# The same start address, 448 modulo 1024 bytes, for every activation operand that streams against the weights of a two-layer decoder trunk

## The chip, the cores and the metric

The kernel runs on one core of one Trainium2 chip. Its time is the device time of one execution in microseconds (us). A core has a matrix engine (TensorE, PE in the rows; PEld is its weight load), two elementwise engines (VectorE, DVE; ScalarE, ACT), GpSimd (POOL) and SyncE (SP), which issues the transfers. They work in parallel and wait for each other through semaphores. On-chip memory (SBUF) has 128 partitions; an address here is the byte offset within a partition. TensorE accumulates into PSUM.

## The reference

Two decoder layers over 256 tokens and 1024 channels, all in float32. Layer 0 mixes with block attention and a state-space scan side by side, layer 1 with a gated delta rule; after each mixer comes a gated feed-forward part and a gated embedding:

```python
for i in range(DEPTH):                      # DEPTH = 2
    h = rmsnorm(x, norm_mix[i])
    x = x + (even_mixer(h, ...) if i % 2 == 0 else gdn_mixer(h, ...))
    h = rmsnorm(x, norm_ffn[i])
    x = x + conv_ffn(h, ...)                # (silu(conv(h @ w_gate)) * (h @ w_up)) @ w_down, width 2816
    x = x + per_layer_embedding(x, p[i], ...)   # sigmoid(rmsnorm(x) @ w_gate) * (p[i] @ w_proj)
```

Every projection is a product of a (channels x tokens) activation with a weight matrix; there are about 34 million weights.

## The kernel before

**Tiling.** Activations lie with channels on the partitions: a 1024-channel activation is 8 tiles of 128 x 256 (channels x tokens), each 1024 bytes per partition. The weights lie in one stream in the order of their use. `piece` loads up to 1024 columns of it (512 KB) into a `raw` buffer and splits it: `whi` is the value rounded to the matmul's fp32r type by ScalarE (line 155), `wlo` the rest by VectorE (line 156). Four buffers each of `raw`, `whi` and `wlo` go round.

**The product.** Activations are split in the same way by `split` (lines 207 to 212) into a high and a low tile. `mm3` (lines 181 to 183) then does three matmuls for each 128 x 128 weight block: high weights with the high tile, high weights with the low tile, low weights with the high tile. The weight block is the stationary operand; the activation tile, 256 columns, is the moving one. Each of the three loads its own weights.

**The moving tiles and their names.** `xh`, `xl`: the normalized residual, 8 pairs (lines 224, 225); they lie in the pool that lives through the whole program, except for the ones that feed the embedding gate (`pgt`), which lie in the feed-forward part's own pool. `yh`, `yl`: the 22 pairs in the middle of the feed-forward part (lines 294, 295). `ah`, `al`: attention's output, 4 pairs (lines 640, 641). `qT`, `kT`, `sl`: the state-space output, 8 pairs, in buffers that held queries and keys before (lines 676, 677). `gh`, `gl`: the delta rule's output, 16 pairs (lines 988, 989). `ph`, `pl`: the embedding's 2 pairs, which take a buffer each of the `whi` and `wlo` rings (lines 318 to 321).

**The outputs.** In PSUM: `pg`, `pu` (gate, up), `pd` (down: 8 tiles of 22 blocks each), `pp` (embedding projection), `pgt` (embedding gate), `pxbc`, `pz`, `pqk` (layer 0's mixer inputs), `pgd`, `pz` (layer 1's), `pwa`, `pws` (layer 0's mixer output from attention and state space), `pwo` (layer 1's mixer output).

**Counts.** 6192 matmuls come from `mm3`. `pg` and `pu`: 2112 in both layers. `pd`: 1056. `pgt`: 384. `pp`: 96. `pwo`: 384, half of them in the middle of the mixer. `pws`: 192. `pwa`: 96. The inputs of the two mixers: 1872.

**Order.** A scheduler puts the instructions in order for each engine; splits of weights are moved ahead of other work (lines 153 to 156).

Of the kernel before, what the change touches and what calls it, by code (L numbers as in the profile page):

```python
# [8 lines left out]
F32R = mybir.dt.float32r  # L9
# [7 lines left out]
P = 128  # L17
BLK = 1024
# [3 lines left out]
T = 256  # L22
D = 1024
KD = D // P
DFF = 2816
NF = DFF // P
# [24 lines left out]
class Trunk:  # L51
    def __init__(self, ctx, tc, stream, xT, pT, pv, tok, cst, out):
# [12 lines left out]
        self.chain = ""  # L65
        self.nrm = ep(tc.tile_pool(name="nrm", bufs=1, space=PSUM))

        warm = self.cpool.tile([P, 1], F32, tag="warm", name="warm")
        nc.vector.memset(warm, 0.0)
        nc.scalar.activation(warm, warm, AF.Exp)  # L70
# [28 lines left out]
    def v(self, name, i=0):  # L99
        o, _ = PV[name]  # L100
        return self.pv[:, o + i:o + i + 1]

    def uid(self, s):
        self.n += 1
        return f"{s}_{self.n}"
# [107 lines left out]


    def norm_begin(self, gain, pool=None):
        self.ngain, self.npool = gain, pool or self.cpool
        self.nss = None
        self.a = [None] * KD

    def norm_tile(self, m, late=False):  # L220
        nc = self.nc
        if m == KD - 1 and not late:
            self.norm_square(m)
        xh = self.npool.tile([P, T], F32R, tag=f"xh{m}", name=self.uid("xh"), bufs=1)
        xl = self.npool.tile([P, T], F32R, tag=f"xl{m}", name=self.uid("xl"), bufs=1)
        self.split(self.x[m], xh, xl, self.v(self.ngain, m))
        self.a[m] = (xh, xl)
        if m < KD - 1 and not late:
            self.norm_square(m)
# [40 lines left out]
    def ffn(self, i, nxt):  # L270
        nc, tc = self.nc, self.tc
        with self.psum(acc=7), tc.tile_pool(name=f"ffn{i}", bufs=3) as fp:
            ys = []
            for f in range(NF):
                wg, wu = self.piece([("ffn_w_gate", i, 0, KD, f * P, P), ("ffn_w_up", i, 0, KD, f * P, P)])
                pg, pu = self.acc("pg"), self.acc("pu")
# [10 lines left out]
                sl = fp.tile([P, T], F32, tag="sl", name=self.uid("sl"))  # L287
# [3 lines left out]
                        nc.scalar.activation(self.zb[0][f], self.ident.unsqueeze(1).to_broadcast([P, 4, P]), AF.Copy)  # L291
                y = fp.tile([P, T], F32, tag="y", name=self.uid("y"))
                nc.vector.tensor_tensor(y, sl, pu[:, :T], op=ALU.mult)
                yh = fp.tile([P, T], F32R, tag=f"yh{f}", name=self.uid("yh"), bufs=1)
                yl = fp.tile([P, T], F32R, tag=f"yl{f}", name=self.uid("yl"), bufs=1)
                self.split(y, yh, yl)
                ys.append((yh, yl))
            self.norm_begin(f"ple{i}", fp)
# [15 lines left out]
    def ple_proj(self, i, pool):  # L314
        nc = self.nc
        raw = self.rawp.tile([P, BLK], F32, tag="raw", name=self.uid("raw"))
        nc.sync.dma_start(raw[:, :2 * T], self.pT[:, i].rearrange("p k t -> p (k t)"))
        ph = self.splp.tile([P, BLK], F32R, tag="whi", name=self.uid("ph"))
        pl = self.splp.tile([P, BLK], F32R, tag="wlo", name=self.uid("pl"))
        self.split(raw[:, :2 * T], ph[:, :2 * T], pl[:, :2 * T])  # L320
        pa = [(ph[:, k * T:(k + 1) * T], pl[:, k * T:(k + 1) * T]) for k in range(2)]
        self.pp = []
        ws = self.piece([("ple_w_proj", i, 0, 2, m * P, P) for m in range(KD)])
        for m in range(KD):
            ps = self.acc("pp")
            self.mm3(ps[:, :T], ws[m], pa)
            t = pool.tile([P, T], F32, tag=f"pp{m}", name=self.uid("pp"), bufs=1)
            nc.scalar.activation(t, ps[:, :T], AF.Copy, scale=0.5)
            self.pp.append(t)
# [84 lines left out]
    def _even(self, mp):  # L414
# [3 lines left out]
        KEEP = lambda shape, tag, dt=F32: mp.tile(shape, dt, tag=tag, name=self.uid(tag), bufs=1)  # L418
# [70 lines left out]
        gm = []  # L489
        for g in range(2):  # L490
# [4 lines left out]
            t = KEEP([P, 3, P], f"gm{g}")  # L495
# [42 lines left out]
        qT, kT = [], []  # L538
# [52 lines left out]
        for k0 in range(0, 8, 2):  # L591
            (wh, wl), = self.piece([(W, 0, k0, 2, 1024, 512)])
            for c in range(2):
                for k in range(2):
                    ah, al = self.a[k0 + k]
# [7 lines left out]


        aA = []
        def attend(hp):
            po = self.nrm.tile([P, 512], F32, tag="nrm", name=self.uid("po"))
            for e in range(2):
# [28 lines left out]
                PE.matmul(po[rows, 0:P], vh(0), pT[:, 0:P], start=True, stop=True)  # L637
                PE.matmul(po[rows, P:T], vh(0), pT[:, P:2 * P], start=True, stop=False)
                PE.matmul(po[rows, P:T], vh(1), pT[:, 2 * P:], start=False, stop=True)
            ah = KEEP([P, T], f"ah{hp}", F32R)  # L640
            al = KEEP([P, T], f"al{hp}", F32R)
            self.split(po[:, :T], ah, al)
            aA.append((ah, al))

# [6 lines left out]
        for g in range(2):  # L651
# [18 lines left out]
            t = self.small(2)  # L670
# [2 lines left out]
            Rg = self.replicate(rg, 2)  # L673
            for m in range(4 * g, 4 * g + 4):
                V.tensor_tensor(ytiles[m], ytiles[m], Rg[:, :T], op=ALU.mult)
                ah = KEEP([P, T], f"qT{m}" if m < 4 else f"kT{m - 4}", F32R)
                al = KEEP([P, T], f"sl{m}", F32R)
                self.split(ytiles[m], ah, al, self.v("snorm", m))
                aS.append((ah, al))

# [22 lines left out]
    def _odd(self, mp):  # L703
# [62 lines left out]

        cw = lambda t: (lambda j: self.v("gcw", t * 4 + j))
        ao = []

        def conv_tile(w, t, dst):  # L770
            ps = self.acc("pgd")
# [212 lines left out]
        def gate(kh, oT, zs):  # L984
            for e in range(2):
                z = zs[e]
                V.tensor_tensor(z, z, oT[:, e * T:(e + 1) * T], op=ALU.mult)
                ah = KEEP([P, T], f"gh{(2 * kh + e) % 16}", F32R)
                al = KEEP([P, T], f"gl{(2 * kh + e) % 16}", F32R)
                self.split(z, ah, al, nh)  # L990
                ao.append((ah, al))

# [151 lines left out]
```

## Time and profile before

| | us |
|---|---|
| median of 3 runs | 938.79 |
| lowest, highest | 937.0, 942.94 |
| the profiled execution's own time | 941.01 |
| its span, first to last instruction | 939.2 |

How to read the rows: a row of the timeline gives the start of an instruction in us from the start of the span, its recorded duration, engine, line, operation, and output tile <- input tiles. Matmuls overlap in the pipeline, so the recorded duration of one (0.28 us) is longer than the distance from its start to the start of the next. That distance is called the pitch here. It is found from two starts that lie far apart and the number of matmuls between them, which the loops give.

### The profile page before, as it was taken

The numbers are of one execution on the slowest core, as the hardware profiler recorded it, in microseconds if no ns is written. First come the engines' busy times: TensorE is split into PE (matmuls) and PEld (weight loads), VectorE is DVE, ScalarE is ACT, GpSimd is POOL, SyncE is SP. The second block draws the span as 40 slices with busy tenths as digits, with TensorE's granted clock in tenths as the row PEclk, the third lists the DMA queues.
The fourth block names the chain that finished last, engine by engine and source line by source line (L and its number), as shares of the span: only waits on it lengthen the run. The fifth ranks groups of instructions, "written<-read, shape, count | busy, mean of one in ns | idle before, by whom it ended". The sixth has DMA issues, their size and how long they took to land.

```text
span 939.2 us, 19988 instructions
## 1 busy us (share of the span) xinstructions
PE 910.0 (97%) x7834; PEld 870.1 (93%) x7834; DVE 750.1 (80%) x1636; ACT 583.7 (62%) x1235; POOL 74.3 (8%) x77
## 2 busy tenths in 40 slices
PE   8999999999999999999899999999999999999997
PEld 6988778999999999988899888988999999999997
DVE  6976778988888666889989999989678777776665
ACT  6576565666655544667688767876656555554452
POOL 0000112100000011012101111011001000000100
PEclk9999999999999999999999999999999999999999
DMA  7543323556656555554422332334445565655561
GB/s 274 183 128 113 113 91 115 158 178 202 195 189 195 180 182 174 184 154 128 146 69 79 103 114 69 111 93 113 136 138 178 180 193 189 183 181 177 172 198 68
DMA packets 40990, 141.40 MB, mean 151 GB/s; under 512 B 4672, under 2 KB 6208, under 8 KB 40896
## 3 DMA queue, kind: packets, MB, share of 16 engines
q1 hardware_dynamic: 40608, 139.84, 48.1%
q8 instruction: 61, 1.00, 0.4%
q10 hardware_dynamic: 288, 0.29, 0.1%
q14 instruction: 33, 0.27, 0.1%
HBM read 139.06 MB, written 1.05 MB: 149 GB/s over the span
## 4 chain that ended last, share of the span: by engine, by line
PE 78%; DVE 15%; ACT 4%; issue 2%; POOL 1%; DMA 0%; POOLq 0%; DVEq 0%
PE pd L183 4%; PE pd L181 4%; PE pd L182 4%; PE pg L181 4%; PE pg L182 4%; DVE wlo L156 4%; PE pu L183 4%; PE pu L182 4%; PE pg L183 4%; PE pu L181 4%; DVE chh L366 2%; PE pgd L181 2%; PE pgd L182 2%; PE pgd L183 2%; PE pwo L182 1%
## 5 line engine op out<-in xcount | busy, mean ns | idle before, releaser
L156 DVE TENSOR_TENSOR wlo<-raw,whi 128x1024 fp32r<-128x1024 f32 (+2 forms) x266 | 322.2, 1212 | 90.5 <-ACT whi L155 88.1
L155 ACT ACTIVATE whi<-raw 128x1024 fp32r<-128x1024 f32 (+2 forms) x266 | 276.5, 1040 | 179.1 <-PE pd L182 44.8
L183 PE MATMUL pd<-yh,wlo 128*128 128x256 f32 x352 | 99.6, 283 | 0.0
L181 PE MATMUL pd<-yh,whi 128*128 128x256 f32 x352 | 99.6, 283 | 0.0
L182 PE MATMUL pd<-yl,whi 128*128 128x256 f32 x352 | 99.6, 283 | 0.0
L181 PE MATMUL pg<-xh,whi 128*128 128x256 f32 x352 | 98.2, 279 | 0.6 <-DVE x L694 0.3
L181 PE MATMUL pu<-xh,whi 128*128 128x256 f32 x352 | 98.2, 279 | 0.0
L182 PE MATMUL pg<-xl,whi 128*128 128x256 f32 x352 | 98.2, 279 | 0.0
L182 PE MATMUL pu<-xl,whi 128*128 128x256 f32 x352 | 98.0, 279 | 0.0
L183 PE MATMUL pu<-xh,wlo 128*128 128x256 f32 x352 | 98.0, 279 | 0.0
L183 PE MATMUL pg<-xh,wlo 128*128 128x256 f32 x352 | 98.0, 279 | 0.0
L181 PE MATMUL pgd<-xh,whi 128*128 128x256 f32 x256 | 76.9, 300 | 0.0
L182 PE MATMUL pgd<-xl,whi 128*128 128x256 f32 x256 | 75.3, 294 | 0.0
L183 PE MATMUL pgd<-xh,wlo 128*128 128x256 f32 x256 | 74.8, 292 | 0.0
L366 DVE SCALAR_TENSOR_TENSOR chh<-cg,pv,chh 128x255 f32<-128x255 f32 x132 | 66.6, 504 | 0.6
L182 PEld LDWEIGHTS pd<-yl,whi 128*128 128x128 f32 x352 | 67.0, 190 | 0.0
L183 PEld LDWEIGHTS pd<-yh,wlo 128*128 128x128 f32 x352 | 67.0, 190 | 0.0
L181 PEld LDWEIGHTS pd<-yh,whi 128*128 128x128 f32 x352 | 67.0, 190 | 0.0
L182 PEld LDWEIGHTS pg<-xl,whi 128*128 128x128 f32 x352 | 66.8, 190 | 0.0
L182 PEld LDWEIGHTS pu<-xl,whi 128*128 128x128 f32 x352 | 66.8, 190 | 0.0
L181 PEld LDWEIGHTS pg<-xh,whi 128*128 128x128 f32 x352 | 66.1, 188 | 0.8 <-issue 0.8
L181 PEld LDWEIGHTS pu<-xh,whi 128*128 128x128 f32 x352 | 66.1, 188 | 0.0
(361 smaller groups left out, 2657.5 us busy)
## 6 DMA issues: line engine op xcount, KB each, us to landing
raw<-stream SPq DMA_DIRECT2D x232, 512.0 KB, 3.6
raw<-stream SPq DMA_DIRECT2D x32, 448.0 KB, 3.2
x<-xT SPq DMA_DIRECT2D x4, 256.0 KB, 4.8
out<-x SPq DMA_DIRECT2D x8, 128.0 KB, 1.9
cst<-cst SPq DMA_DIRECT2D x1, 645.0 KB, 6.0
raw<-pT SPq DMA_DIRECT2D x2, 256.0 KB, 2.5
pv<-pv ACTq DMA_DIRECT2D x1, 215.5 KB, 4.5
raw<-stream SPq DMA_DIRECT2D x1, 128.0 KB, 3.2
```

The source lines that it names most:

```text
L155: nc.scalar.activation(hi[:, :cols], raw[:, :cols], AF.Copy)
L156: self.lo_engine(lo).tensor_tensor(lo_[:, :cols], raw[:, :cols], hi[:, :cols].bitcast(F32), op=ALU.subtract)
L181: nc.tensor.matmul(out, wh, ah, start=start and k == 0, stop=False)
L182: nc.tensor.matmul(out, wh, al, start=False, stop=False)
L183: nc.tensor.matmul(out, wl, ah, start=False, stop=stop and k == n - 1)
L366: nc.vector.scalar_tensor_tensor(out=h[:, s:], in0=g[:, :T - s], scalar=w(3 - s), in1=h[:, s:], op0=ALU.mult, op1=ALU.add)
```

## The change

A helper `moving` allocates one tile for a whole set of moving operands, aligned to 1024 bytes, and hands out pieces that begin 448 bytes into it and follow each other at 1024 bytes. So each piece begins at 448 modulo 1024. It is used for the long-lived `xh`/`xl` (now one tile `xx`), the embedding gate's (`xp`), the feed-forward middle (`yy`), the embedding operand (`pa`), the outputs of layer 0's mixer (`am`) and of layer 1's (`gm`).

```diff
+        self.xx = self.moving(self.cpool, 2 * KD, "xx")
...
+    def moving(self, pool, n, tag):
+
+        t = pool.tile([P, 112 + n * T], F32R, tag=tag, name=self.uid(tag), bufs=1, align_bytes=1024)
+        return [t[:, 112 + i * T:112 + (i + 1) * T] for i in range(n)]
...
-        self.ngain, self.npool = gain, pool or self.cpool
+        self.ngain = gain
+        self.nx = self.moving(pool, 2 * KD, "xp") if pool else self.xx
...
-        xh = self.npool.tile([P, T], F32R, tag=f"xh{m}", name=self.uid("xh"), bufs=1)
-        xl = self.npool.tile([P, T], F32R, tag=f"xl{m}", name=self.uid("xl"), bufs=1)
+        xh, xl = self.nx[2 * m:2 * m + 2]
...
+            yy = self.moving(fp, 2 * NF, "yy")
...
-                yh = fp.tile([P, T], F32R, tag=f"yh{f}", name=self.uid("yh"), bufs=1)
-                yl = fp.tile([P, T], F32R, tag=f"yl{f}", name=self.uid("yl"), bufs=1)
+                yh, yl = yy[2 * f:2 * f + 2]
...
-        ph = self.splp.tile([P, BLK], F32R, tag="whi", name=self.uid("ph"))
-        pl = self.splp.tile([P, BLK], F32R, tag="wlo", name=self.uid("pl"))
-        self.split(raw[:, :2 * T], ph[:, :2 * T], pl[:, :2 * T])
-        pa = [(ph[:, k * T:(k + 1) * T], pl[:, k * T:(k + 1) * T]) for k in range(2)]
+        pa = self.moving(pool, 4, "pa")
+        pa = [pa[0:2], pa[2:4]]
+        for k in range(2):
+            self.split(raw[:, k * T:(k + 1) * T], *pa[k])
...
-            ah = KEEP([P, T], f"ah{hp}", F32R)
-            al = KEEP([P, T], f"al{hp}", F32R)
+            ah, al = am[2 * hp:2 * hp + 2]
...
-                ah = KEEP([P, T], f"qT{m}" if m < 4 else f"kT{m - 4}", F32R)
-                al = KEEP([P, T], f"sl{m}", F32R)
+                ah, al = am[8 + 2 * m:10 + 2 * m]
...
-                ah = KEEP([P, T], f"gh{(2 * kh + e) % 16}", F32R)
-                al = KEEP([P, T], f"gl{(2 * kh + e) % 16}", F32R)
+                ah, al = gm[4 * kh + 2 * e:4 * kh + 2 * e + 2]
```

Where the allocator puts the operands, in bytes modulo 1024, in the two built programs:

| operand | feeds | before | now |
|---|---|---|---|
| `xh`, `xl` (long-lived) | `pg`, `pu`, both mixers' inputs | 448 | 448 |
| `yh`, `yl` | `pd` | 256 | 448 |
| `xh`, `xl` (embedding gate) | `pgt` | 256 | 448 |
| `ph`, `pl` | `pp` | 512 | 448 |
| `gh`, `gl` | `pwo` | 544 | 448 |
| `ah`, `al` | `pwa` | 288 | 448 |
| `qT`, `kT` with `sl` | `pws` | 448 or 960, with 288 | 448 |
| weight blocks in `whi`, `wlo` (stationary) | all | 512 or 0 | 480 or 992 |

The number of matmuls and their operands stay. The order of the engines' work changes only around the embedding of each layer, in the same way in both. The first place is TensorE in layer 0's embedding gate, where `rep`, the transposes that spread the normalizing factor `rtok` over the partitions, stand among the `pgt` matmuls. Before:

```order
L181 MATMUL pgt_5236<-xh_4962,whi_5196 128x256
L182 MATMUL pgt_5236<-xl_4963,whi_5196 128x256
L183 MATMUL pgt_5236<-xh_4962,wlo_5197 128x256
L263 MATMUL rep_5184<-cst,rtok_5161 128x128 x2
L181 MATMUL pgt_5236<-xh_5060,whi_5196 128x256
L182 MATMUL pgt_5236<-xl_5061,whi_5196 128x256
L183 MATMUL pgt_5236<-xh_5060,wlo_5197 128x256
```

With the change (line 263 is now 269, lines 181 to 183 are 187 to 189):

```order
L188 MATMUL pgt_5123<-xp_4203,whi_5085 128x256
L189 MATMUL pgt_5123<-xp_4203,wlo_5086 128x256
L187 MATMUL pgt_5123<-xp_4203,whi_5085 128x256
L269 MATMUL rep_5073<-cst,rtok_5050 128x128 x2
L188 MATMUL pgt_5123<-xp_4203,whi_5085 128x256
L189 MATMUL pgt_5123<-xp_4203,wlo_5086 128x256
L187 MATMUL pgt_5123<-xp_4203,whi_5085 128x256
```

`rep` moved 17 matmuls forward: it stood before the last block of the second output tile's eight and stands now within the second block.

The second place is VectorE at the same layer's last down-projection tiles: `pl`, the low part of the embedding operand. Before:

```order
L156 TENSOR_TENSOR wlo_5004<-raw_5001,whi_5003 128x896
L156 TENSOR_TENSOR wlo_5031<-raw_5028,whi_5030 128x896
L306 TENSOR_TENSOR d_4959<-pd_4874,Rrep_2609 128x256
L307 TENSOR_TENSOR x<-x,d_4959 128x256
L208 TENSOR_TENSOR pl_5067<-raw_5064,ph_5066 128x512
L211 SCALAR_TENSOR_TENSOR xl_4963<-x,pv,xh_4962 128x256
L156 TENSOR_TENSOR wlo_5073<-raw_5070,whi_5072 128x1024
L156 TENSOR_TENSOR wlo_5079<-raw_5076,whi_5078 128x1024
```

With the change (line 208 is now 214, 156 is 162):

```order
L217 SCALAR_TENSOR_TENSOR xp_4203<-x,pv,xp_4203 128x256
L214 TENSOR_TENSOR pa_4954<-raw_4952,pa_4954 128x256 x2
L162 TENSOR_TENSOR wlo_4894<-raw_4891,whi_4893 128x896
L162 TENSOR_TENSOR wlo_4921<-raw_4918,whi_4920 128x896
L312 TENSOR_TENSOR d_4851<-pd_4766,Rrep_2555 128x256
L313 TENSOR_TENSOR x<-x,d_4851 128x256
```

The one split of 512 columns is now two of 256, and stands two weight splits earlier; ScalarE's high part moved likewise, and SyncE issues its load one piece of weights earlier in the same way. Two weight splits that stood between the steps that make `rtok` now come after it.

## Rows read from the trace of the kernel before

**Rows 1.** Granted clock of the core.
```profile
core 0: 939.2 us, clock 0.997
```
**Rows 2.** The page: busy time and share by engine, then the chain's shares.
```profile
PE 910.0 (97%) x7834; PEld 870.1 (93%) x7834; DVE 750.1 (80%) x1636; ACT 583.7 (62%) x1235; POOL 74.3 (8%) x77
...
PE 78%; DVE 15%; ACT 4%; issue 2%; POOL 1%; DMA 0%; POOLq 0%; DVEq 0%
```
**Rows 3.** Stretches: length; busy us (count) of PE, PEld, DVE, ACT, POOL; clock, DMA, GB/s.
```profile
192.00:313.30 121.30, 120.98 (x1066) 120.92 (x1067) 98.40 (x167) 75.84 (x118) 0.00 (x0) 1.00 0.60 190
313.30:383.20 69.90, 69.90 (x586) 69.90 (x584) 43.03 (x53) 35.01 (x52) 5.63 (x6) 1.00 0.58 182
408.60:658.50 249.90, 235.22 (x2296) 221.28 (x2297) 230.35 (x662) 184.84 (x517) 32.72 (x25) 1.00 0.35 105
715.40:840.70 125.30, 125.30 (x1065) 125.30 (x1066) 98.20 (x165) 71.72 (x112) 0.00 (x0) 1.00 0.59 183
```
**Rows 4.** Timeline, TensorE, layer 0 gate/up: start us, us, instruction.
```profile
201.81 0.28 PE L181 MATMUL pu<-xh,whi 128*128 128x256 f32 x1
...
310.61 0.28 PE L181 MATMUL pu<-xh,whi 128*128 128x256 f32 x1
```
**Rows 5.** Timeline, TensorE, layer 0 down projection.
```profile
321.23 0.28 PE L181 MATMUL pd<-yh,whi 128*128 128x256 f32 x1
...
368.75 0.28 PE L181 MATMUL pd<-yh,whi 128*128 128x256 f32 x1
```
**Rows 6.** Timeline, TensorE, layer 1 gate/up.
```profile
721.97 0.28 PE L181 MATMUL pg<-xh,whi 128*128 128x256 f32 x1
...
837.87 0.28 PE L181 MATMUL pu<-xh,whi 128*128 128x256 f32 x1
```
**Rows 7.** Timeline, TensorE, layer 1 down projection.
```profile
848.62 0.28 PE L181 MATMUL pd<-yh,whi 128*128 128x256 f32 x1
...
896.13 0.28 PE L181 MATMUL pd<-yh,whi 128*128 128x256 f32 x1
```
**Rows 8.** Timeline, TensorE, layer 0 embedding gate.
```profile
389.60 0.28 PE L181 MATMUL pgt<-xh,whi 128*128 128x256 f32 x1
...
401.12 0.28 PE L181 MATMUL pgt<-xh,whi 128*128 128x256 f32 x1
```
**Rows 9.** Timeline, TensorE, output projection of layer 1's mixer.
```profile
692.00 0.28 PE L181 MATMUL pwo<-gh,whi 128*128 128x256 f32 x1
...
708.80 0.28 PE L181 MATMUL pwo<-gh,whi 128*128 128x256 f32 x1
```
**Rows 10.** Timeline, TensorE, output projection of layer 0's mixer, SSM part.
```profile
177.31 0.28 PE L181 MATMUL pws<-qT,whi 128*128 128x256 f32 x1
...
188.83 0.28 PE L181 MATMUL pws<-qT,whi 128*128 128x256 f32 x1
```
**Rows 11.** Timeline, TensorE, four starts of columns in layer 0's mixer.
```profile
27.12 0.28 PE L181 MATMUL pxbc<-xh,whi 128*128 128x256 f32 x1
...
29.95 0.28 PE L181 MATMUL pxbc<-xh,whi 128*128 128x256 f32 x1
...
36.81 0.28 PE L181 MATMUL pxbc<-xh,whi 128*128 128x256 f32 x1
...
39.53 0.28 PE L181 MATMUL pqk<-xh,whi 128*128 128x256 f32 x1
```
**Rows 12.** Timeline, TensorE, warm-up matmuls merged (count at the end).
```profile
5.83 0.93 PE L76 MATMUL pwarm<-zt 128*128 128x256 f16 x7
```
**Rows 13.** Timeline, VectorE then TensorE, the normalizing factor in layer 0's embedding.
```profile
388.70 0.16 DVE L199 SCALAR_TENSOR_TENSOR rtok<-rt,ry 128x2 f32<-128x2 f32 x1
...
389.01 0.40 PE L263 MATMUL rep<-cst,rtok 128*128 128x128 f32 x2
```
**Rows 14.** Timeline, ScalarE then VectorE, splits of the embedding operand, layer 0.
```profile
368.88 0.63 ACT L207 ACTIVATE ph<-raw 128x512 fp32r<-128x512 f32 x1 [1.56 <-PE pd L182]
...
369.75 0.68 DVE L208 TENSOR_TENSOR pl<-raw,ph 128x512 fp32r<-128x512 f32 x1
```

More of the change, by code (lines that the diff above doesn't have):

```diff
@@ L605, in _even @@
         aA = []
+        am = self.moving(mp, 24, "am")
         def attend(hp):
@@ L768, in _odd @@
         ao = []
+        gm = self.moving(mp, 32, "gm")
         def conv_tile(w, t, dst):
```

## The prediction

> **What bounds the kernel.** I looked at the clock first: 0.997 of full speed [rows 1], so TensorE runs at its 2.4 GHz level almost throughout and the clock is not the subject. Then at the shares: TensorE is busy 97% of the span and holds 78% of the chain that ends last [rows 2]. Then at stretches [rows 3]. In the feed-forward parts (first, second and fourth row) TensorE is busy without a gap while VectorE has 20 to 40% to spare; there, a nanosecond off each matmul comes straight off the time. In layer 1's mixer (third row) VectorE is busy 230.35 of 249.9 us and TensorE has holes of 14.7; there a faster matmul buys little.
>
> Busy time does not show how fast TensorE runs, since matmuls overlap; the pitch does. Divide the distance of two starts by the matmuls between them:
>
> - Layer 0 gate/up, 20 column tiles of 48 matmuls: 108.80 us / 960 = **113.3 ns** [rows 4].
> - Layer 0 down, 6 tiles of 66: 47.52 / 396 = **120.0 ns** [rows 5].
> - Layer 1 gate/up, 984 matmuls: 115.90 / 984 = **117.8 ns** [rows 6].
> - Layer 1 down: 47.51 / 396 = **120.0 ns** [rows 7].
> - Embedding gate, 4 tiles of 24: 11.52 / 96 = **120.0 ns** [rows 8].
> - Mixer outputs: layer 1, 16.80 / 144 = **116.7 ns** [rows 9]; layer 0, 11.52 / 96 = **120.0 ns** [rows 10].
> - Layer 0's mixer input, 24 matmuls each: 2.83 / 24 = 117.9 ns, and ten us later 2.72 / 24 = 113.3 ns [rows 11].
>
> All of these are the same instruction, 256 columns at the full clock. Set beside the table of addresses: operands at 256 stream at 120.0; at 544 at 116.7; at 448 at 113.3 or 117.8; the mixture of 448, 960 and 288 at 120.0. The address goes with the pitch, with one flaw that matters most here: at 448, same code and same tile, there are **two** steady pitches, and a stretch keeps its own for over 100 us [rows 4, 6]. Since rows 11 show both within 13 us, I take it that a restart after a pause picks one.
>
> **The change, part by part.** Nothing is added to or taken from TensorE's work. What may change is the pitch of 2208 of 6192 matmuls (1056 down, 96 embedding projection, 384 gate, 384 + 192 + 96 mixer outputs). A matmul at 120.0 saves 6.67 ns if it comes to 113.3, and 2.22 if to 117.8.
>
> *Down and embedding projection*, 576 a layer, follow gate/up without a pause, so I give them the pitch of their layer as it was: layer 0, 576 x 6.67 = 3.84 us; layer 1, 576 x 2.22 = 1.28 us. Bounds: both layers fast 7.7, both slower 2.6, nothing if the address is not the cause. The projection's rows are not shown; I give it down's price.
>
> *Embedding gate*, 192 a layer, starts anew after the norm: the mean of both prices, 192 x 4.44 = 0.85 a layer, 1.7 in all (bounds 0.9 and 2.6).
>
> *Layer 0's mixer output*: 192 at 120.0, again 0.85 (bounds 0.4 and 1.3); the 96 from attention I price at a tenth of a us, like an operand at 544, since 288 has the same remainder by 256.
>
> *Layer 1's mixer output*: 192 back to back at 116.7 either win 3.3 ns or lose 1.1 each, +0.64 or -0.21; I take 0.2. The other 192 stand among VectorE's work in the mixer (third row of [rows 3]): nothing.
>
> *Embedding operand.* Its split of 512 columns, 0.63 us on ScalarE and 0.68 on VectorE [rows 14], becomes two of 256, perhaps 0.2 us more on each, two layers; the cover is VectorE's spare time in the second row of [rows 3], 69.9 - 43.0 us. It also stands earlier and frees a weight buffer; that buffer would matter only if TensorE waited for weights there, which it doesn't. Price: 0.
>
> *`rep` 17 matmuls earlier.* TensorE would reach it some 17 x 0.12 = 2.0 us sooner. `rtok` starts at 388.70 and lasts 0.16, and `rep` at 389.01 [rows 13], so it came just behind it. But two weight splits of 1024 columns leave the chain to `rtok`; at up to twice the 0.68 of the one of 512 [rows 14] they take up to 2.7 us. Both ends move alike: 0, bounds 0.5 won and 1 lost a layer. Queued behind `rep` are the rest of the gate's matmuls, and VectorE waits for the spread factor; both shift with it.
>
> *Long-lived `xh`/`xl`* stay at 448: gate/up and the mixers' inputs keep their two pitches. But which one a layer draws is drawn again: 1056 matmuls x 4.44 = 4.7 us for gate/up, and 576 x 4.44 = 2.6 for what follows, **7.2 us a layer**.
>
> The sum, with one layer fast and one slower as now: 3.84 + 1.28 + 1.7 + 0.85 + 0.1 + 0.2 = 8.0 us. From the profiled execution's own 941.01 this gives **933 us**. That execution is 2.2 above the median of 938.79; the runs lie between 937.0 and 942.94, a spread that one layer's draw would cover.
>
> **A rule that speaks against it.** The warm-up matmuls, of another type but with 256 columns too, follow each other at (0.93 - 0.28) / 6 = 0.108 us [rows 12]; the streams above are all slower. The Trainium skill, TensorE: Matmul & The Clock Gate, section "Wait — 56ns, not 53.3ns?", gives start to start as columns / 2.4 GHz plus 2.5 ns: 109.2 ns for 256 columns, whatever the address. It fits the warm-up and not the three slower pitches. By it the change would move no pitch and the sum would be 0.
>
> **The rivals.**
>
> *Both layers draw the fast pitch.* 933 - 7.2 - 0.9 (the gate's other half) = 925 us. For it: the lowest run, 937.0, lies 4.0 below the profiled one, about what a fast gate/up in layer 1 would give, so I take a fast draw for somewhat the likelier, six in ten. Against: it needs two.
>
> *Both draw the slower.* 933 + 7.2 = 940 us: down's gain is given back by layer 0's gate/up.
>
> *The address is not the cause,* as by the rule above. Down has blocks of 8, 7 and 7 per load, and its stage differs from gate/up in every other respect as well; then the time stays at 939 to 941. Against it: layer 0's and layer 1's down agree to 0.1 ns [rows 5, 7] while gate/up before them differ by 4.5.
>
> *The weights' address costs more than the operands' gains.* The new tiles push the weight rings from 512 to 480 modulo 1024, so each block now starts 32 bytes off a multiple of 64. The distance from weight block to moving operand was 0, 32 or 64 modulo 128 in every stream; now it is 96 in all. No row shows that. If the pair decides and not the moving operand alone, all streams would come to the slowest steady pitch seen, 120.0: layer 0 gate/up + 1056 x 6.67 = 7.0, layer 1 + 1056 x 2.22 = 2.3, mixers' inputs 1872 x 0 to 4.9 ns, half of 9 as part is hidden, 4.5; down and gate stay. 941 + 13.8 = **955 us**, slower. It decides the sign where the mean pitch of the feed-forward parts passes today's: (1056 x 113.3 + 1056 x 117.8 + 1152 x 120.0) / 3264 = 117.1 ns. For it: a mixture of two addresses already gave 120 where one of them alone gives 113 [rows 4, 10], so more than one address counts. Against it: weights alternate between 512 and 0 in every stream and the steady pitches don't alternate.
>
> **How the numbers follow.** Forecast, one layer fast and one slower, 933: 42%. Both fast, 925: 27%. Both slower, 940: 12%. Address not the cause, 940: 8%. Weights' address, 955: 11%. Given one layer each, the small terms and the mixers' own draws (1872 matmuls, up to 4.44 ns each, part of it hidden) spread it over some 926 to 939. A measurement of this kernel tells about 1% from no change, so faster means under 929.4 and slower over 948.2. Faster: all of the second case and a quarter of the first, its tail below 929.4: 0.27 + 0.11 = 0.38. Slower: the last case and a remnant, 0.12. Within 1%: 0.50. The range runs from 920 (both fast, with every small term at its better bound) to 944 (both slower with the small terms lost); it leaves out the last case and some of the second.
>
> **What would show it.** In the timeline after: `pd` at 113.3 or 117.8 and no longer 120.0, in the pitch of the gate/up just before; `pgt` and `pws` likewise; `pwo` no longer 116.7. The two layers' feed-forward parts shorter by what their pitch says and no new idle time of TensorE in them. `rep` with no wait over 0.5 us. Wrong: `pd` still at 120.0 (address not the cause); a pitch that no stretch had before, above all in gate/up, whose operand kept its address (the weights' address); both layers at one pitch (the draw, not the mechanism).

## The result, and the profile after

The change made the kernel slower: 946.22 us, the median of 6 runs (945.64 to 948.71), against 937.89 of the kernel before (6 runs, 935.62 to 942.94). The ratio is 1.0084, 95% interval 1.0059 to 1.0108. That is 0.8% slower, inside the 1% that the prediction called no change, but on the wrong side of it: the forecast was 933.0 with a range to 944. The runs also lie closer together: 3.1 us from lowest to highest instead of 7.3.

Read the profile after in the order of the one before. The clock and the page's shares come first:

```profile
core 0: 944.4 us, clock 0.999
```
```profile
PE 916.6 (97%) x7834; PEld 876.9 (93%) x7834; DVE 752.1 (80%) x1638; ACT 584.1 (62%) x1237; POOL 74.9 (8%) x77
...
PE 80%; DVE 13%; ACT 3%; issue 1%; DMA 1%; POOL 1%; SPq 0%; POOLq 0%; ACTq 0%; DVEq 0%
```

The clock is 0.999 (before 0.997 [rows 1]) and TensorE is as full as before: 97%, 80% of the chain [rows 2]. Nothing new is waited for: outside its busy time TensorE has 27.8 us of the span, before 29.2. The busy time itself grew by 6.6 us, for the same 7834 matmuls. The stretches (length; busy us and count of PE, PEld, DVE, ACT, POOL; clock) say where:

```profile
193.30:319.20 125.90, 125.87 (x1064) 125.90 (x1065) 98.11 (x165) 74.99 (x118) 0.00 (x0) 1.00 0.58 182
319.20:388.20 69.00, 69.00 (x586) 69.00 (x585) 44.52 (x55) 35.95 (x54) 5.89 (x6) 1.00 0.62 192
413.10:664.00 250.90, 236.83 (x2296) 222.90 (x2297) 230.50 (x662) 185.14 (x517) 32.64 (x25) 1.00 0.34 104
721.20:847.10 125.90, 125.89 (x1064) 125.90 (x1065) 98.20 (x165) 71.77 (x112) 0.00 (x0) 1.00 0.59 182
```

Against [rows 3]: layer 0's gate/up took 121.30 us (0.6 of it ahead of the first gate matmul) and takes 125.90; the stage behind it (down and embedding projection) went from 69.90 to 69.00, less than the 3.84 that I had summed; layer 1's gate/up 125.30 to 125.90. In these three TensorE is busy to the last tenth, so the lengths are the matmuls' own pitch. The timeline gives it (start us, recorded us, engine, line, instruction), two starts for each of layer 0's mixer output (96 matmuls between them), gate/up (912), down (396) and embedding gate (96), and of layer 1's mixer output (144) and gate/up (912):

```profile
178.16 0.28 PE L187 MATMUL pws<-am,whi 128*128 128x256 f32 x1
...
189.53 0.28 PE L187 MATMUL pws<-am,whi 128*128 128x256 f32 x1
...
202.82 0.28 PE L187 MATMUL pu<-xx,whi 128*128 128x256 f32 x1
...
310.74 0.28 PE L187 MATMUL pu<-xx,whi 128*128 128x256 f32 x1
...
327.06 0.28 PE L187 MATMUL pd<-yy,whi 128*128 128x256 f32 x1
...
373.93 0.28 PE L187 MATMUL pd<-yy,whi 128*128 128x256 f32 x1
...
394.51 0.28 PE L187 MATMUL pgt<-xp,whi 128*128 128x256 f32 x1
...
405.87 0.28 PE L187 MATMUL pgt<-xp,whi 128*128 128x256 f32 x1
...
697.57 0.28 PE L187 MATMUL pwo<-gm,whi 128*128 128x256 f32 x1
...
714.61 0.28 PE L187 MATMUL pwo<-gm,whi 128*128 128x256 f32 x1
...
730.70 0.28 PE L187 MATMUL pu<-xx,whi 128*128 128x256 f32 x1
...
838.62 0.28 PE L187 MATMUL pu<-xx,whi 128*128 128x256 f32 x1
```

Six times the same number: 11.37 / 96 = 118.4 ns, 107.92 / 912 = 118.3, 46.87 / 396 = 118.4, 11.36 / 96 = 118.3, 17.04 / 144 = 118.3, 107.92 / 912 = 118.3. The four pitches of before, 113.3 [rows 4], 117.8 [rows 6], 120.0 [rows 5, 7, 8, 10] and 116.7 [rows 9], are gone. What was slower than 118.3 became faster, as meant; but gate/up, the largest stream, became slower although its moving operand kept its address. Of its two operands in SBUF only the weights moved, to 480 modulo 1024 from 512.

By stages, each from its first matmul's start in the timeline to the next one's, in us (one execution of each kernel):

| stage | before | after | difference |
|---|---|---|---|
| first instruction to layer 0 gate/up | 192.64 | 193.33 | +0.7 |
| layer 0 gate/up | 120.69 | 125.93 | +5.2 |
| layer 0 down, projection, gate | 95.31 | 93.85 | -1.5 |
| layer 1's mixer | 306.71 | 308.10 | +1.4 |
| layer 1 gate/up | 125.34 | 125.93 | +0.6 |
| layer 1 down, projection, gate | 98.54 | 97.26 | -1.3 |
| span | 939.23 | 944.40 | +5.2 |

The profiled execution of before drew the fast pitch in layer 0's gate/up and the slower one in layer 1's; where it drew the fast one, the change loses most.

### The profile page after: what moved, and what is told of

Its sections match the earlier page's. It is cut to its first block, busy times and chain, and to the rows that moved or that the text cites. A ratio compares the mean times of both kernels' runs of the same rounds, so it can differ in the third digit from the quotient of the medians.

```text
span 944.4 us, 19992 instructions
## 1 busy us (share of the span) xinstructions
PE 916.6 (97%) x7834; PEld 876.9 (93%) x7834; DVE 752.1 (80%) x1638; ACT 584.1 (62%) x1237; POOL 74.9 (8%) x77
## 4 chain that ended last, share of the span: by engine, by line
PE 80%; DVE 13%; ACT 3%; issue 1%; DMA 1%; POOL 1%; SPq 0%; POOLq 0%; ACTq 0%; DVEq 0%
PE pg L187 4%; PE pg L188 4%; PE pd L189 4%; PE pu L189 4%; PE pu L188 4%; PE pu L187 4%; PE pd L187 4%; PE pg L189 4%; PE pd L188 4%; DVE wlo L162 4%; DVE chh L372 2%; PE pgd L187 2%; PE pgd L189 2%; PE pgd L188 2%; PE pwo L188 2%; PE pwo L187 2%
## 5 line engine op out<-in xcount | busy, mean ns | idle before, releaser
L187 PE MATMUL pg<-xx,whi 128*128 128x256 f32 x352 | 99.0, 281 | 0.6 <-DVE x L1004 0.3
L187 PE MATMUL pu<-xx,whi 128*128 128x256 f32 x352 | 99.1, 281 | 0.0
L188 PE MATMUL pg<-xx,whi 128*128 128x256 f32 x352 | 99.1, 281 | 0.0
L189 PE MATMUL pu<-xx,wlo 128*128 128x256 f32 x352 | 98.9, 281 | 0.0
L189 PE MATMUL pd<-yy,wlo 128*128 128x256 f32 x352 | 98.9, 281 | 0.0
L188 PE MATMUL pd<-yy,whi 128*128 128x256 f32 x352 | 98.9, 281 | 0.0
L187 PE MATMUL pd<-yy,whi 128*128 128x256 f32 x352 | 98.9, 281 | 0.0
L189 PE MATMUL pg<-xx,wlo 128*128 128x256 f32 x352 | 98.9, 281 | 0.0
L188 PE MATMUL pu<-xx,whi 128*128 128x256 f32 x352 | 98.9, 281 | 0.0
L187 PE MATMUL pgd<-xx,whi 128*128 128x256 f32 x256 | 77.2, 302 | 0.0
L188 PE MATMUL pgd<-xx,whi 128*128 128x256 f32 x256 | 75.5, 295 | 0.0
L187 PEld LDWEIGHTS pg<-xx,whi 128*128 128x128 f32 x352 | 66.3, 188 | 0.8 <-issue 0.8
L188 PEld LDWEIGHTS pg<-xx,whi 128*128 128x128 f32 x352 | 66.3, 188 | 0.0
L187 PEld LDWEIGHTS pu<-xx,whi 128*128 128x128 f32 x352 | 66.3, 188 | 0.0
L188 PEld LDWEIGHTS pu<-xx,whi 128*128 128x128 f32 x352 | 66.3, 188 | 0.0
L188 PEld LDWEIGHTS pd<-yy,whi 128*128 128x128 f32 x352 | 66.3, 188 | 0.0
L187 PEld LDWEIGHTS pd<-yy,whi 128*128 128x128 f32 x352 | 66.3, 188 | 0.0
```

The lines of the kernel that those rows point to most:

```text
L187: nc.tensor.matmul(out, wh, ah, start=start and k == 0, stop=False)
L188: nc.tensor.matmul(out, wh, al, start=False, stop=False)
L189: nc.tensor.matmul(out, wl, ah, start=False, stop=stop and k == n - 1)
```

## The experiments

**The weight rings put back.** The rings are the four buffers each of `whi` and `wlo`. The theory: weights' and moving operand's addresses together set the pitch. The rival: something else in the new layout does (one tile for many pieces, its dependences). A pad of 32 bytes in the pool of the two rings puts them at 512 again; the moving operands stay at 448, and nothing else of the change is edited:

```diff
         self.smallp = ep(tc.tile_pool(name="smallp", bufs=3))
+        self.splp.tile([P, 8], F32, tag="pad", name="pad", bufs=1)
```

> The changed kernel with a pad of 32 bytes ahead of the two weight rings: they go from 480 back to 512 modulo 1024, the moving operands stay at 448, nothing else is edited. If the weights' address (alone or with the moving one) cost the time: the steady 118.3 ns is gone, every stream is at 113.3 or 117.8, and the time is the one I forecast for the change, 925 to 940, about 933. If it was the new layout of the moving pieces in one tile, or the dependences of that tile: 118.3 ns stays everywhere and the time stays at 946 within 2.

Measured: 934.1 us (10 runs, 925.63 to 936.86), ratio 0.9909 (0.9878 to 0.9941) to the kernel before, which ran at 940.58 beside it. The pitch of the down projection, layer 0 and then layer 1, 396 matmuls each:

```profile
320.80 0.28 PE L188 MATMUL pd<-yy,whi 128*128 128x256 f32 x1
...
365.68 0.28 PE L188 MATMUL pd<-yy,whi 128*128 128x256 f32 x1
...
845.20 0.28 PE L188 MATMUL pd<-yy,whi 128*128 128x256 f32 x1
...
891.84 0.28 PE L188 MATMUL pd<-yy,whi 128*128 128x256 f32 x1
```

44.88 / 396 = 113.3 ns and 46.64 / 396 = 117.8: the two pitches of 448 against 512 are back, one in each layer, and `pd` now has its layer's. Thirty-two bytes of pad decide between 946 and 934. The layout in one tile isn't what the change lost by.

**The rings alone, in the kernel before.** The reverse edit: pads in the kernel before move the two rings to 480; every moving operand keeps its address but `ph` and `pl`, which lie in the rings. Together or alone? If the weights' address alone counted, all streams would read 118.3.

```diff
         self.smallp = ep(tc.tile_pool(name="smallp", bufs=3))
+        self.splp.tile([P, 248], F32, tag="pad", name="pad", bufs=1)
+        self.smallp.tile([P, 8], F32, tag="pad2", name="pad2", bufs=1)
```

> The kernel before with pads that put the two weight rings alone from 512 to 480 modulo 1024; every moving operand keeps its address. If the two addresses set the pitch together: gate, up and the mixers' inputs (moving 448) go to 118.3 ns and cost about 8 us, the down projections and the embedding gates (moving 256) go from 120.0 to the 116.7 ns that the difference of 32 had before, 4.7 us less; in all about +3 us, 941. If the weights' address alone: 118.3 ns everywhere, the down projections and gates give back 2.4 us, in all about +6 us, 944. If the weights' address does nothing: 113.3 or 117.8 and 120.0 as before, 938.

Measured: 946.54 us (7 runs, 944.91 to 946.88), ratio 1.0070 (1.0043 to 1.0097). The time is near that of the changed kernel, by other pitches; no moving operand of the change is needed for the loss. Its rows are those of the theory of the pair: gate/up (moving 448, 912 matmuls), down (256, 396), embedding projection (480, since `ph` lies in the ring; 42):

```profile
202.18 0.28 PE L183 MATMUL pu<-xh,whi 128*128 128x256 f32 x1
...
310.10 0.28 PE L183 MATMUL pu<-xh,whi 128*128 128x256 f32 x1
...
326.32 0.28 PE L183 MATMUL pd<-yh,whi 128*128 128x256 f32 x1
...
372.52 0.28 PE L183 MATMUL pd<-yh,whi 128*128 128x256 f32 x1
...
380.22 0.28 PE L183 MATMUL pp<-ph,whi 128*128 128x256 f32 x1
...
385.26 0.28 PE L183 MATMUL pp<-ph,whi 128*128 128x256 f32 x1
```

107.92 / 912 = 118.3 ns, 46.20 / 396 = 116.7, 5.04 / 42 = 120.0: three pitches in one kernel with one weights' address. I had expected 941 by the pair and 944 by the weights alone; the pitches say the pair, but the median lies 2.5 us above even the second. The two profiled executions are 3.9 apart, near the +3: gate/up +5.8, down, projection and gates -4.1, layer 1's mixer and its output +2.2, by first starts as above; 1.2 of this last belongs to the clock (see the mixers below). That execution is the lowest of its seven. The two runs at a granted clock of 0.998 and 0.997 took 944.91 and 945.26, the five at 0.995 and 0.996 took 946.42 to 946.88: most of what the median has above the trace goes with the clock and not with an address.

**The pairs by themselves.** A kernel that leaves the model out and keeps only bursts of `mm3` at 64 pairs of addresses:

```diff
+            for k in range(KD):
+                a = lambda t: t[:, wo + k * P:wo + (k + 1) * P]
+                b = lambda i: mv[:, mo + i * T:mo + (i + 1) * T]
+                nc.tensor.matmul(ps[:, :T], a(wh), b(2 * k), start=r == 0 and k == 0, stop=False)
+                nc.tensor.matmul(ps[:, :T], a(wh), b(2 * k + 1), start=False, stop=False)
+                nc.tensor.matmul(ps[:, :T], a(wl), b(2 * k), start=False, stop=r == 1 and k == KD - 1)
```

> The model is left out; only TensorE's stream is kept: bursts of 48 fp32r matmuls of 256 columns in the order of mm3 (weight high x moving high, weight high x moving low, weight low x moving high, over eight blocks), weights stepping 512 bytes and moving pieces 1024 bytes, each burst after a pause for its eviction. 64 pairs of start addresses: weights at 0, 16, ... 112 and moving pieces at 0, 16, ... 112 modulo 128, each pair twice. Theory A (the two addresses together set the pitch, by their difference moving minus weights modulo 128): 113.3 or 117.8 ns wherever the difference is 64, 120.0 at 0, 116.7 at 32, 118.3 at 96, in every row of weights. Theory B (the weights' address alone): a row with weights at 96 is at 118.3 for all moving addresses, a row with weights at 0 holds 113.3 to 120.0. Theory C (the moving address alone, so that the lost time came from elsewhere): every row of weights reads alike, 120.0 at moving 0, 116.7 at 32, 113.3 or 117.8 at 64.

Four bursts of it, the 24th and the 48th start of each. The letters give the addresses in steps of 16 bytes from a = 0: weights 0, moving 32; weights 64, moving 0; both 64; weights 96, moving 64, the pair of the changed kernel:

```profile
52.77 0.28 PE L50 MATMUL wamc<-mv,wl 128*128 128x256 f32 x1
...
55.57 0.28 PE L50 MATMUL wamc<-mv,wl 128*128 128x256 f32 x1
...
247.05 0.28 PE L50 MATMUL wema<-mv,wl 128*128 128x256 f32 x1
...
249.77 0.28 PE L50 MATMUL wema<-mv,wl 128*128 128x256 f32 x1
...
272.85 0.28 PE L50 MATMUL weme<-mv,wl 128*128 128x256 f32 x1
...
275.73 0.28 PE L50 MATMUL weme<-mv,wl 128*128 128x256 f32 x1
...
375.89 0.28 PE L50 MATMUL wgme<-mv,wl 128*128 128x256 f32 x1
...
378.73 0.27 PE L50 MATMUL wgme<-mv,wl 128*128 128x256 f32 x1
```

2.80 / 24 = 116.7 ns, 2.72 / 24 = 113.3, 2.88 / 24 = 120.0, 2.84 / 24 = 118.3. The pairs at steps of 32 bytes, mean pitch in ns over the last 39 matmuls (both bursts of a pair agreed):

| weights at | moving 0 | 32 | 64 | 96 |
|---|---|---|---|---|
| 0 | 120.0 | 116.6 | 117.8 | 120.1 |
| 32 | 118.4 | 120.0 | 116.6 | 117.8 |
| 64 | 113.3 | 118.4 | 120.0 | 116.6 |
| 96 | 117.3 | 113.3 | 118.4 | 120.0 |

The diagonals are constant, so the difference counts: theory A, and B and C are out. With weights at odd multiples of 16 the diagonals are nearly constant too, but on values of their own (118.3 at difference 0, 119.9 at -32, 113.3 at 64; one pair, weights 48 and moving 0, read 123.2). So the difference alone sets the pitch only among weights at multiples of 32, as all weights of the kernels here are. And my modulus was wrong. Moving minus weights = 64 gives 117.8 and -64 gives 113.3; these are the same modulo 128 and differ modulo 256, and so do 96 (120.1) and -32 (118.4). Eight more bursts of this run, weights at 0 and moving at 64, 192, 320 and so on to 960, read 117.8 and 113.3 in turn: the pattern repeats every 256 bytes.

**Does the pause choose?** Bursts again, weights at 0, moving at 16 addresses modulo 256, each eight times (this kernel too leaves the model out). The code puts one matmul of another length, `pre`, ahead of each burst:

```diff
+            nc.tensor.matmul(pre[:, :32 + 28 * s], wh[:, :P], mv[:, :32 + 28 * s], start=True, stop=True)
+            burst("s" + LET[s] + "m" + LETTERS[j], 0, j * STEP)
```

> The model is left out again: bursts of 48 matmuls as in the first grid, weights at 0 modulo 1024, moving pieces at 0, 16, ... 240 modulo 256, each address eight times, each burst led by one matmul of another length (32, 60, ... 228 columns) so that the stream begins in another phase. If a pair of addresses has one pitch and the two of 448 against 512 come from the pause before the stream: the same eight values at most addresses (120.0 at 0 and 128, 116.6 at 32), and a mix of 113.3 and 117.8 at 64 and 192. If bit 7 of the address chooses between the two (the first run had 117.8 at 64, 320, 576 and 832 and 113.3 at 192, 448, 704 and 960): eight times 117.8 at 64 and eight times 113.3 at 192. An address with 113.3 in all eight would be the one to lay the streams at: 16 and 112 had it in the first run.

The trace has another order than the code. Nothing waits for `pre`, and all 128 of them stand early: one to eight in a row between the warm-up bursts and before each of the first 45 others, none before the remaining 83, which begin behind a pause. Both sorts at moving 64, three `pre` ahead of the burst `same` and the first matmul of `sdme`:

```profile
63.06 0.43 PE L59 MATMUL pre<-mv,wh 128*128 128x88 f32 x3
...
373.27 0.38 PE L49 MATMUL sdme<-mv,wh 128*128 128x256 f32 x1 [0.53 <-ACT res L52]
```

So an address has two or three bursts led by `pre` in different ways, and five or six with the same beginning. The steady pitch of the last 24 matmuls, and in how many of the eight bursts:

| moving at | ns | moving at | ns |
|---|---|---|---|
| 0 | 120.0 | 128 | 118.8 |
| 16 | 113.3 (6), 118.6 (2) | 144 | 116.7 (5), 118.7 (3) |
| 32 | 116.7 (6), 117.8 (2) | 160 | 117.2 (6), 118.7 (2) |
| 48 | 118.3 | 176 | 119.2 to 119.4 |
| 64 | 117.8 (6), 113.3 (2) | 192 | 113.3 |
| 80 | 120.0 (6), 118.3 (2) | 208 | 119.2 |
| 96 | 120.0 | 224 | 118.3 |
| 112 | 113.3 | 240 | 117.0 to 117.3 |

Two bursts at 64, led by three `pre` of 88 columns and by two of 144 and 172, show the draw (24th and 48th start):

```profile
66.47 0.28 PE L51 MATMUL same<-mv,wl 128*128 128x256 f32 x1
...
69.19 0.28 PE L51 MATMUL same<-mv,wl 128*128 128x256 f32 x1
...
169.54 0.28 PE L51 MATMUL sbme<-mv,wl 128*128 128x256 f32 x1
...
172.37 0.28 PE L51 MATMUL sbme<-mv,wl 128*128 128x256 f32 x1
```

2.72 / 24 = 113.3 ns and 2.83 / 24 = 117.9, the same burst, the same addresses. The other burst at 113.3 was led too (200 and 228 columns); the five without `pre` all read 117.8. At the other addresses as well the bursts without `pre` agree among themselves to 0.2 ns, but for two that stand in a row: 144 behind a pause of 0.82 us instead of 0.53, and 160 right behind it. So the way a stream begins can choose its pitch, at some differences. At 112 and 192 it didn't here, in three led beginnings and the common one. All 32 pairs of the first grid whose weights lie at a multiple of 32 agree with this table by their difference modulo 256, to 0.13 ns; those with weights at 16, 48, 80 or 112 mostly don't. The kernels do too: 448 against 480 is 224, 118.3; 256 against 512 is 0, 120.0; 544 against 512 is 32, 116.7. One thing doesn't: 448 against 512 is 192, in all eight bursts 113.3 here, and in the kernels also 117.8 for whole layers [rows 6].

**The slowest difference, in the kernel.** One number of the change, so that the difference is 0:

```diff
-        t = pool.tile([P, 112 + n * T], F32R, tag=tag, name=self.uid(tag), bufs=1, align_bytes=1024)
-        return [t[:, 112 + i * T:112 + (i + 1) * T] for i in range(n)]
+        t = pool.tile([P, 120 + n * T], F32R, tag=tag, name=self.uid(tag), bufs=1, align_bytes=1024)
+        return [t[:, 120 + i * T:120 + (i + 1) * T] for i in range(n)]
```

> The changed kernel with one number changed: the moving pieces start at 480 modulo 1024 (120 elements of pad instead of 112), the weight rings stay at 480. If the difference of the two addresses sets the pitch (0 here, as in the first grid where 0-0, 32-32, 64-64 and 96-96 all read 120.0): 120.0 ns in every stage, 1.7 ns more than the change on the 5,000 or so of the 6,192 matmuls that stand in the path, +8.5 us, about 955. If the weights' address alone makes 118.3: nothing moves, 946.

Measured: 953.05 us (4 runs, 952.8 to 953.66), ratio 1.0177 (1.0162 to 1.0192). Layer 0 gate/up, 912 matmuls:

```profile
203.41 0.28 PE L187 MATMUL pu<-xx,whi 128*128 128x256 f32 x1
...
312.85 0.28 PE L187 MATMUL pu<-xx,whi 128*128 128x256 f32 x1
```

109.44 / 912 = 120.0 ns, in each long stream. Against the change's 946.22 it is 6.8 us (spans 951.2 against 944.4), where I had put 8.5: layer 1's mixer hardly answers to the pitch (below). This is the pitch that I had given the rival of the weights' address.

**The fast difference, in the kernel, two ways.** Difference 112: rings at 512 and moving pieces at 112 (the first experiment's pad, and 28 in place of the change's 112 elements), or rings left at 480 and moving pieces at 336 (84 elements alone).

> The changed kernel with the rings back at 512 (32 bytes of pad) and the moving pieces at 112 modulo 1024 (28 elements of pad instead of 112): the difference is 112 modulo 256, at which the second run of bursts had 113.3 in eight beginnings of eight, whatever came before. If that holds in the kernel: 113.3 ns in every stage, no draw; against the profiled run of the rings at 512 alone (934.3, layer 1's feed-forward block and embedding gates, 1,785 matmuls, at 117.8) 4.45 ns less on these and some in the mixers, 8 to 11 us less: 923 to 926, and a spread of the runs as small as the change's. If a draw stays at this address: 925 to 937 as with the rings at 512. If only the difference modulo 128 counted in the sense of the first grid (117.0 at 32-16, 64-48, 96-80): 117, about 938.

> The changed kernel with one number changed: the moving pieces start at 336 modulo 1024 (84 elements of pad instead of 112), the weight rings stay at 480; the difference is 112 modulo 256, as in the kernel with 512 and 112. If the difference modulo 256 is all that counts: 113.3 ns in every stage and the same time as that kernel, 923 to 926. If each address counts by itself too: another pitch, 117 to 118.3, 938 to 946.

Measured: 928.98 us (4 runs, 928.21 to 930.87), ratio 0.9922 (0.9907 to 0.9937), and 928.17 us (4 runs, 927.3 to 928.52), ratio 0.9908 (0.9892 to 0.9925); the kernel before ran at 936.63 beside them. Layer 1's gate/up, where a slow draw had stood, 912 matmuls, with rings at 512 and then at 480:

```profile
721.31 0.28 PE L188 MATMUL pu<-xx,whi 128*128 128x256 f32 x1
...
824.67 0.28 PE L188 MATMUL pu<-xx,whi 128*128 128x256 f32 x1
...
721.33 0.28 PE L187 MATMUL pu<-xx,whi 128*128 128x256 f32 x1
...
824.68 0.28 PE L187 MATMUL pu<-xx,whi 128*128 128x256 f32 x1
```

103.36 / 912 = 113.3 ns, 103.35 / 912 = 113.3. All long streams of both kernels stand at 113.3, and the two agree within 0.1 us in every feed-forward stage although neither operand has the same address in both: it is the difference. Their spans are both 926.4, 7.9 less than the 934.3 of the profiled execution with 512 and 448: 4.6 in layer 1's gate/up, 2.6 in its down and projection, 0.7 behind them, and nothing in the mixers. I had set 923 to 926 by taking 8 to 11 from that span, while a run's time is 1.8 us longer than its span. Both beat the kernel before and the change. Their ratios overlap that of 512 and 448, whose runs stand in two groups, four from 925.63 to 928.85 and six from 933.89 to 936.86; what difference 112 takes away is the second group. The "whatever came before" of the first expectation went further than the bursts, which had three led beginnings and a common one; the narrow runs of the two kernels fit it.

**High and low apart.** Bursts (model left out) with the high and the low pieces at addresses of their own, 256 pairs, weights at 0:

```diff
+            b = lambda o, i: mv[:, o + i * T:o + (i + 1) * T]
+            nc.tensor.matmul(ps[:, :T], a(wh), b(hi, 2 * k), start=k == 0, stop=False)
+            nc.tensor.matmul(ps[:, :T], a(wh), b(lo, 2 * k + 1), start=False, stop=False)
+            nc.tensor.matmul(ps[:, :T], a(wl), b(hi, 2 * k), start=False, stop=k == KD - 1)
```

> The model is left out: bursts of 24 matmuls, both weight tiles at 0 modulo 1024, the high pieces of the moving operand at 0, 16, ... 240 and the low pieces at 0, 16, ... 240 modulo 256 on their own, 256 pairs. If 113.3 ns is the floor of this stream at any address: no pair under 113.3, and pairs of two good addresses (112 or 192) at 113.3. If it is only the best of equal addresses: some pair lies under 113.3, down to what one column a cycle of 2.4 GHz would give for 256 columns, an estimate of 106.7.

Over the last 12 matmuls of each burst: no pair under 113.3 ns, three at 113.3 (both at 64, at 112, at 192), nine from 115.6 to 115.8, the other 244 from 116.7 to 121.2. Mixing two good addresses, 112 and 192, gave 115.6 or 120.0, not 113.3. In this form of stream 113.3 is the best that was found, and only with high and low at the same address.

## Why the prediction was wrong

**The step that failed** is "*Long-lived `xh`/`xl`* stay at 448: gate/up and the mixers' inputs keep their two pitches". They did not: 118.3 in both layers' gate/up, and 118.1 to 118.4 in the mean for the mixers' inputs (neighbouring starts within a tile). The step reads the pitch from the moving operand's address alone. That the weights move from 512 to 480 stood in the table of addresses and under the rivals, and there it got 11%. The pair decides, and the step covers gate/up's 2112 matmuls and the mixers' 1872, of 6192. In place of its 0 gate/up lost 5.8 us. The same assumption priced the gains: at 118.3 instead of 113.3 or 117.8 they came to 2.5 us of the 8.0 forecast (last column below).

**Why the rival was priced too low in chance.** The argument against it was that weights alternate between 512 and 0 in every stream while the pitches don't alternate. True, and no evidence: the pattern repeats every 256 bytes (the eight bursts above), and 512 and 0 are the same in it. A step of the weights that keeps the remainder cannot show whether the remainder matters. The argument for it, that a mixture of moving addresses gave 120.0 where one of them alone gives 113 [rows 10], was right: against 512 that operand's high pieces lie at 192 and its low ones at 32, and the bursts with 192 and 32 read 120.0 too. What the profile before did hold is that all of its weights had one remainder; so it could not tell "the moving address" from "the difference", and nothing in it justified odds of eight to one.

**Its price.** 955 us rested on 120.0 ns for all; the pair had 118.3. At 120.0, difference 0, the kernel took 953.05. So the sum of the rival was right to 2 us for a case that did not occur, and its sign was right for the one that did. Its two gate/up terms held there (7.0 and 2.3 as forecast); the mixers' 4.5 came to 3.2, and its "0 to 4.9 ns" follows from none of the pitches, which would give 2.2 or 6.7. The point from which it decides, 117.1 ns as the mean of the feed-forward parts, held: 118.3 is above it.

**The terms of the sum**, with the rings put back at 512, which is the case that the forecast described. The profiled execution drew as before, fast in layer 0 and slower in layer 1:

| term | forecast | measured, rings at 512 | measured, the change |
|---|---|---|---|
| down + projection, layer 0 | -3.84 | -3.8 (69.91 to 66.09) | -0.9 |
| down + projection, layer 1 | -1.28 | -1.3 (69.93 to 68.66) | -1.0 |
| embedding gates | -1.7 | -1.1 | -0.8 |
| layer 0's mixer output, SSM | -0.85 | -0.8 (24.39 to 23.55) | -0.2 |
| layer 1's mixer output | -0.2 | -0.6 | +0.4 |
| gate/up, both layers | 0 | 0.0 | +5.8 |

With the rings at 512 they add up to -7.6, against -7.9 forecast for the same terms. The span of that execution fell by only 5.0: its first matmul of the mixer came 0.8 us later, and layer 1's mixer took 1.9 us more, most of it by the clock (below). That the median of ten runs of this kernel, 934.1, stands by the forecast 933.0 is in part luck: the sum started from one execution, and the median falls where six of ten runs drew the slower group. That a stream's start address sets its pitch was right, and so were nearly all prices; that the weights' address counts as much was what it left out.

**The draw** was right where the difference stays 192: rings at 512, one layer each in the trace, and runs in two groups where I had 925 and 933 (none of ten at 940). At the same granted clock they are 7 to 8 us apart: 926.24 against 933.89 and 934.31 at 1.000, 928.85 against 936.08 at 0.995. That the lower group is fast in both layers is inferred from its times; no trace was taken of it. At 224 every burst had the same pitch, led or not, which fits the narrow runs after the change.

**The mixers.** I gave layer 1's mixer nothing, and that nearly held: it took 249.9 us before, 250.9 in the change at 118.3 and 251.3 at 120.0. The other four executions took 251.7 to 251.9 whatever their pitch, and most of what makes them longer isn't an address. With the pieces at 112: the whole stretch, then its first matmul, a piece of it and the piece behind:

```profile
403.90:655.70 251.80, 237.03 (x2296) 222.51 (x2297) 230.50 (x662) 185.22 (x517) 32.85 (x25) 0.99 0.34 104
...
403.87 0.28 PE L188 MATMUL pab<-xx,whi 128*32 128x256 f32 x1 [2.03 <-DVE pleg L350]
...
405.10:408.30 3.20, 3.20 (x16) 2.44 (x15) 2.15 (x7) 1.44 (x4) 0.68 (x1) 0.50 0.62 191
408.60:411.80 3.20, 3.20 (x29) 3.18 (x29) 1.87 (x11) 1.55 (x4) 0.00 (x0) 1.00 0.00 0
```

VectorE's busy time is that of before (230.35 [rows 3]), and so are TensorE's holes, 14.8 us after 14.7. But the granted clock is 0.50 in one piece, the level of 1.2 GHz, and 16 matmuls stand in it where the next one holds 29. TensorE had been idle for 2.03 us ahead of the mixer, then busy. The traces of all four executions have such a piece in this mixer; those of before, of the change and of 120.0 have none. Against the same matmuls of the kernel before, the mixer falls 1.2 to 1.4 us behind across that piece and is 1.8 to 2.0 late at its end. The other 0.5 to 0.8 us is open.

**`rep` and the embedding operand**, priced at 0, cost nothing. The normalizing factor and its spread, and the operand's two splits:

```profile
391.59 0.16 DVE L205 SCALAR_TENSOR_TENSOR rtok<-rt,ry 128x2 f32<-128x2 f32 x1
...
391.90 0.40 PE L269 MATMUL rep<-cst,rtok 128*128 128x128 f32 x2
```
```profile
368.51 0.72 ACT L213 ACTIVATE pa<-raw 128x256 fp32r<-128x256 f32 x2 [0.45 <-DMA raw<-pT]
...
369.38 0.75 DVE L214 TENSOR_TENSOR pa<-raw,pa 128x256 fp32r<-128x256 f32 x2
```

`rep` starts 3.67 us after the gate's first matmul (388.23) where it was 5.77 [rows 13], 17 matmuls earlier as the order said, 0.31 behind `rtok` as before, and no idle time stands in its row. The splits take 0.72 and 0.75 us instead of 0.63 and 0.68 [rows 14], and TensorE is busy 69.00 of 69.00 us there.

**The rule that was weighed.** The Trainium skill, TensorE: Matmul & The Clock Gate, section "Wait — 56ns, not 53.3ns?", gives start to start as columns / 2.4 GHz plus 2.5 ns and names no address; for 256 columns that is an estimate of 109.2 ns. All four pitches of before lie 4 to 11 ns above it, the fastest too, which the prediction's "three slower pitches" passes over. Three address pads, at one clock, gave 113.3, 118.3 and 120.0 in the same kernel; the measurements decide here, and none of 256 pairs came under 113.3. The same skill's SBUF — State Buffer, section "Operand start alignment", holds which start addresses are legal and gives them no time; all of those used here are legal, and they differ by 5.9%.

## What to carry to other kernels

If matmuls stream without a gap, measure the start-to-start distance of each long stream; where the same form has several, look at the start addresses of both operands, and at their difference modulo 256 bytes (with the weights at multiples of 32). Any edit that changes the size of a pool moves everything that is allocated behind it: list the addresses of all operands, not only of those the edit is about, before you call a stream untouched. A constant factor in the profile (here: all weights at one remainder) cannot be excluded as a cause by that profile.

## What the runs showed of the hardware

The pitch of a 256-column fp32r matmul whose weights change each time lay between 113.3 and 120.0 ns at differences of 0 to 224 in steps of 32, with weights at multiples of 32 bytes; a fast one (113.3) beside a slow one (119.2) only 16 bytes away (192 and 208). At some differences two steady pitches exist, and what precedes the stream chooses: bursts with the same beginning agreed, others of the same addresses didn't. Why the difference acts so is not shown by these runs. The Trainium skill, SBUF — State Buffer, section "A bandwidth-pool intuition that's wrong (but worth ruling out)", lists a read port of its own for the weight load, independent of the moving operand's; if nothing else joined the two, their difference would do nothing, and it makes 5.9%. What chooses 117.8 over 113.3 in the kernel at a difference of 192, where every burst drew 113.3, stays open too.

The profiled executions also differ at the start. The first six us of the mixer's stream, with the pieces at 112 and in the change:

```profile
8.00:14.00 6.00, 5.43 (x32) 3.91 (x33) 5.36 (x11) 5.94 (x15) 0.00 (x0) 0.72 0.99 382
```
```profile
8.00:14.00 6.00, 4.96 (x39) 4.01 (x40) 5.03 (x10) 5.90 (x15) 0.00 (x0) 1.00 1.02 365
```

The granted clock is a mean of 0.72 in one, part of the stretch at 1.2 GHz and part at 2.4, and 1.00 in the other, 2.4 GHz throughout; the first holds 32 matmuls instead of 39, 0.8 us of work at 118.3 ns. The kernel before has 0.68 and 0.75 in the two halves of that stretch too. Differences of an us between two executions are therefore not put down to addresses here; what brings the clock down, there and in layer 1's mixer, was not followed up.
